# A two-layer decoder trunk on one core: eight small products of the gates and of the compressed keys, each set in one run on TensorE

## The chip, the core and the metric

The kernel runs on one core of a Trainium2 chip. Its engines work side by side, each through its own list of instructions in order: TensorE (PE in the profile; its loads of weights stand apart as PEld), VectorE (DVE), ScalarE (ACT), GpSimd (POOL), and SyncE (SP), which here only issues loads and stores. The metric is the device time of one execution in microseconds (us); less is better. The profile comes from one further execution, recorded instruction by instruction.

## What is computed

The input is x with 512 positions of 1024 numbers, all in float32. Layer 0 normalises x, projects it once, and feeds the columns to two groups of heads: a chunked mLSTM with 4 heads, and a sparse attention with 8 query heads in two groups. Layer 1 is a gated linear recurrence. Two small parts of layer 0 matter here. The first is the gates of the mLSTM, which per chunk of 128 positions need a running maximum of the input gate over the decayed forget gate:

```
bcum = jnp.cumsum(fj, axis=-1)
D = jnp.where(causal, bcum[..., :, None] - bcum[..., None, :] + ij[..., None, :], -jnp.inf)
inter = bcum + m[..., None]
m_row = jnp.maximum(jnp.max(D, axis=-1), inter)
...
m_new = jnp.maximum(bL + m, jnp.max(dl, axis=-1))
```

The second is the compressed keys and values of the attention, two small matrices behind each other with a GELU between them:

```
def compress(blocks, w1, w2):
    flat = blocks.reshape(*blocks.shape[:3], CMP_LEN * NSA_HEAD_DIM)
    return jax.nn.gelu(flat @ w1) @ w2
...
k_cmp = compress(heads(kc, G)[:, :, cmp_idx] + ck_pos, ck_w1, ck_w2)
k_cmp = partial_rope(rms_norm(k_cmp, k_norm[0]), cmp_end)
v_cmp = compress(heads(vc, G)[:, :, cmp_idx] + cv_pos, cv_w1, cv_w2)
```

## The kernel before

The large projections take most of PE's time. Each float32 operand is split into a high and a low part (`whi`, `wlo` for weights, `h0h`, `h0l` for activations), and a product is three PE products of 128 x 128 weights with 512 columns: high by high, high by low, low by high. They add up in PSUM tiles named `mm` (three of them). Weights come from memory in 512 KB pieces (`raw`), ACT rounds a piece to `whi`, DVE subtracts to get `wlo`; there are four buffers of each, so a new piece is converted when PE has left an old one.

The work around the projections hangs in generators, one for each small task. `cg_evac` takes the first group of columns (compressed keys and gates) out of PSUM and starts `kc_t`, `compress` and `gates`. `nq_evac` and `nkv_evac` take out queries and keys and start `prep_q(i)` and `prep_k(i)` for each block i of 128 positions: squares on ACT (`sqj`), a root on POOL (`qrs`, `krs`), a scaling and a rotation on DVE (`x`), four transposes on PE, and the split into high and low parts (`q`, `kd`). `cmp_sm(i)` multiplies the queries of block i with the compressed keys (`kcd`) and makes a softmax of the scores (`sc`, `ce`).

The two tasks that the change touches are these. In `gates()` (line 1117) the scans over `ar` leave running maxima in `rows` (the half `cmx`), and `mrow` holds the carried maximum of the four chunks. `Mr`, the other half of `rows`, is the larger of the two, in lines 1157 to 1159 with one step on DVE for each chunk. Then lines 1169 to 1172 put five products into the PSUM tile `gp`: `on4` by `bd` (32 columns), and four that turn `Mr` into columns (4 rows deep, 128 weight columns, 4 moving columns). In `compress()` (line 1052) `hk` and `h4`, both in the buffer `gb`, are the outputs of the GELU, and lines 1078 to 1081 multiply them with `w2`: one product of 64 weight columns for the keys, two of 128 for the values of two groups. A float32 product that isn't split takes two passes on PE. Both tasks, the transposes of `prep_q` and `prep_k` and others share the two PSUM buffers `tp`. Behind the products come `Mc` (out of `gp`), and `kr`, `vbk`, `kn`, `kh` and `kcd` (the keys on their way to the scores).

No engine runs the program in the order in which it is written. `Plan` records every operation with a price, and `Plan.schedule` sorts each stage six times by these prices, by what an operation waits for, and by how urgent it is; the best order is then issued from line 408. So all instructions carry line 408 in the profile, and they are told apart by the names of their tiles. Products may be tied: lines 249 to 257 set `a.next = b` for two PE products written one behind the other if they fill the array from different columns on with the same load, and the scheduler then issues `b` right behind `a`. The first of a chain takes over what the others wait for. The eight products above were not tied.

Of the kernel before, what the change touches and what calls it, by code (L numbers as in the profile page):

```python
# [158 lines left out]

class Op:  # L160
    __slots__ = ("eng", "fn", "a", "k", "cost", "acc", "pred", "succ", "left", "ready", "start", "end", "done", "late", "after",
                 "load", "cols", "idx", "first", "tiles", "tab", "next")


class Plan:
# [37 lines left out]
    def add(self, eng, fn, a, k, cost):  # L203
        o = Op()
        o.eng, o.fn, o.a, o.k, o.cost, o.idx = eng, fn, a, k, cost, len(self.ops)
        o.pred, o.succ, o.acc, o.tiles, o.first = {}, {}, [], [], []
        o.tab = self.TAB.get(a[2]) if eng == "A" and len(a) > 2 else None
        o.load, o.cols = k.pop("_pe", (0.0, ()))
        o.after = k.pop("_after", None)
        o.next = None  # L210
        aps = [(x, j == 0) for j, x in enumerate(a) if isinstance(x, bass.AP)]
        aps += [(x, n == "accum_out") for n, x in k.items() if isinstance(x, bass.AP)]
        for x, w in aps:
            n = x.tensor.name
            if n in self.tag:
                o.acc.append((n, *((1, 0, 1) if n[:3] in PSUMS else self.region(x)), w))
        self.ops.append(o)


    def edges(self):  # L220
        for o in self.ops:
            for n, m, p0, p1, w in o.acc:
                h = self.hist.get(n)
                if h is None:
                    h = self.hist[n] = []
                if n not in self.tag:
                    pass
                elif n not in self.born:
                    o.first.append(n)
                    self.order.setdefault(self.tag[n], []).append(n)  # L230
                    self.born[n] = o
                elif self.born[n] is not o:
                    o.pred.setdefault(self.born[n], -self.born[n].cost)
                for q, qm, q0, q1, qw in h:
                    if q is not o and (w or qw) and q0 < p1 and p0 < q1 and qm & m:
                        raw = qw and not w
                        lat = self.LAT[q.eng] if raw or q.eng != o.eng else 0.0
                        if q.eng == "T" == o.eng:
                            lat = -q.cost
                        o.pred[q] = max(o.pred.get(q, lat), lat)  # L240
            for n, m, p0, p1, w in o.acc:
                h = self.hist[n]
                if w:
                    h[:] = [x for x in h if x[1] & ~m or x[2] < p0 or x[3] > p1]
                h.append((o, m, p0, p1, w))
            o.tiles = list({x[0] for x in o.acc if x[0] in self.tag})
            if o.after is not None:
                o.pred.setdefault(o.after, -o.after.k.get("_ns", 0.0))
        for a, b in zip(self.ops, self.ops[1:]):
            if a.eng == "T" == b.eng and len(a.cols) < 4 and a.load == b.load and a.cols[0] < b.cols[0]:  # L250
                a.next = b
        for b, a in list(zip(self.ops, self.ops[1:]))[::-1]:
            if b.next:
                for q, lat in a.pred.items():
                    if q is not b:
                        b.pred[q] = max(b.pred.get(q, lat), lat)
                a.pred = {b: -b.cost}
        for o in self.ops:
            for q, lat in o.pred.items():
                q.succ[o] = lat  # L260
# [168 lines left out]
class Mark:  # L429
    t = None  # L430
# [186 lines left out]
def build(tc, I, out):  # L617
# [6 lines left out]
    with ExitStack() as ctx:  # L624
# [42 lines left out]
        def cut(t, shape, p=slice(0, 128)):  # L667
            n = 1
            for d in shape:
                n *= d  # L670
            v = t[p, :n]
            if len(shape) == 1:
                return v
            ls = "abcdef"[:len(shape)]
            return v.rearrange("p (" + " ".join(ls) + ") -> p " + " ".join(ls), **dict(zip(ls, shape)))
# [284 lines left out]
        with ExitStack() as c0:  # L960
# [91 lines left out]
            def compress():  # L1052
# [25 lines left out]
                T.matmul(p[:64, :64], hk, w2[:, 0, :], start=True, stop=True, skip_group_check=True)  # L1078
                for g in range(2):
                    T.matmul(p[:, 64 + 64 * g:128 + 64 * g], flat(h4[:, g]), w2[:, 1, :], start=True, stop=True,  # L1080
                             skip_group_check=True)
                b_end()
                kr = s_t("kr", [64, 64], 1)
                V.tensor_copy(kr, p[:64, :64])
# [32 lines left out]
            def gates():  # L1117
# [36 lines left out]
                V.tensor_copy(aL, cust(cmx, [[128, 4]], 127))  # L1154
                V.tensor_tensor_scan(mrow[:, 1:5], aL, bL, 0.0, op0=OP.max, op1=OP.add)
                Mr = rows[:, 1, :]
                for t in range(4):
                    V.tensor_scalar(Mr[:, 128 * t:128 * (t + 1)], cmx[:, 128 * t:128 * (t + 1)], mrow[:, t:t + 1], None,
                                    op0=OP.max)
                ML = s_t("ML", [4, 2, 4], 1)  # L1160
                V.tensor_tensor(ML[:, 0, :], aL, mrow[:, :4], op=OP.max)
                V.tensor_copy(ML[:, 1, :], mrow[:, :4])
# [6 lines left out]
                T.matmul(gp[:, 16:48], on4, flat(bd), start=True, stop=True, skip_group_check=True)  # L1169
                for t in range(4):  # L1170
                    T.matmul(gp[:, 4 * t:4 * t + 4], Mr[:, 128 * t:128 * (t + 1)], shc("id", 4, 4),
                             start=True, stop=True, skip_group_check=True)
                Mc = s_t("Mc", [128, 48], 1)
                V.tensor_copy(Mc, gp[:, :48])
                V.scalar_tensor_tensor(ex[:, :16], aa, LNS, Mc[:, 16:32], op0=OP.add, op1=OP.subtract)
# [960 lines left out]
```

## Time and profile before

| what | us |
|---|---|
| timed runs, median of 3 | 616.07 (616.03 to 616.64) |
| the profiled execution | 618.45 |
| its span, first to last instruction | 616.7 |
| PE busy in the span | 608.3 (99%) |
| DVE busy | 456.9 (74%) |
| ACT busy | 332.4 (54%) |
| POOL busy | 106.2 (17%) |

The profiled execution takes somewhat longer than the timed ones. Its span leaves out what lies before the first and behind the last instruction. A product counts as busy until its last column has left the array, while the next has long begun; how fast PE works is read from the distance between starts.

### The profile page before, as it was taken

To read this page: it belongs to the slowest core of one execution; us is meant where nothing else is said; L and a number is where in the kernel's file an instruction comes from. 1 tells how busy PE (TensorE), PEld (TensorE's weight loads), DVE (VectorE), ACT (ScalarE), POOL (GpSimd) and SP (SyncE) were. 2 spreads that over 40 slices of the span, in tenths; PEclk is the share of its full clock that TensorE was granted. 3 is DMA by queue.
4 is the path that set the end of the run, shared out by engine and by line. 5 is a ranking of instruction groups with operands and counts; after the bars stand their busy time and mean duration, and the time that the engine had idled before them with its cause. 6 is when DMAs were issued, how large, how long until landed. Compare 5 with 4: busy or idle time off the path is not lost.

```text
span 616.7 us, 11759 instructions
## 1 busy us (share of the span) xinstructions
PE 608.3 (99%) x4482; PEld 490.4 (80%) x4482; DVE 456.9 (74%) x980; ACT 332.4 (54%) x870; POOL 106.2 (17%) x143
## 2 busy tenths in 40 slices
PE   8999999999999999999999999999999999999997
PEld 8877787877778777888888887788877877788886
DVE  5876998698899766566745679997588798996441
ACT  7564465667777664373534756446527365565300
POOL 1441532102002002063012111023000100122100
PEclk9997999999999999999999999999999999999999
DMA  8723133809409407925343524473222215473111
GB/s 321 262 107 103 51 98 127 338 4 222 189 18 299 95 2 179 238 72 213 96 160 120 170 72 135 132 231 118 69 71 70 70 39 168 142 281 126 35 73 64
DMA packets 23528, 82.91 MB, mean 134 GB/s; under 512 B 3376, under 2 KB 4272, under 8 KB 20656
## 3 DMA queue, kind: packets, MB, share of 16 engines
q1 hardware_dynamic: 20880, 65.09, 32.1%
q0 software_dynamic: 2304, 16.78, 10.4%
q8 instruction: 35, 0.57, 0.4%
q10 hardware_dynamic: 288, 0.30, 0.2%
q14 instruction: 21, 0.17, 0.1%
HBM read 77.96 MB, written 20.97 MB: 160 GB/s over the span
## 4 chain that ended last, share of the span: by engine, by line
PE 89%; DVE 5%; issue 2%; DMA 1%; POOL 1%; ACT 1%; DVEq 0%; ACTq 0%; POOLq 0%
PE mm L408 32%; PE mx L408 18%; PE my L408 15%; PE sc L408 7%; PE ac L408 5%; PE tp L408 5%; PE tq L408 5%; PE sd L408 2%; DMA raw<-in_wall_dram 1%; DVE wlo L408 1%; DVE x L408 1%; POOL qk L408 1%; DVE ce L408 0%; POOL krs L408 0%; DVE q L408 0%
## 5 line engine op out<-in xcount | busy, mean ns | idle before, releaser
L408 ACT ACTIVATE whi<-raw 128x512 fp32r<-128x512 f32 (+1 forms) x184 | 104.9, 615 | 83.2 <-PE my L408 30.1
L408 DVE TENSOR_TENSOR wlo<-raw,whi 128x1024 fp32r<-128x1024 f32 (+1 forms) x96 | 114.3, 1197 | 33.0 <-ACT whi L408 32.7
L408 PE MATMUL mm<-whi,h0l 128*128 128x512 f32 (+1 forms) x168 | 68.3, 407 | 0.0
L408 PE MATMUL mm<-whi,h0h 128*128 128x512 f32 (+1 forms) x168 | 68.2, 409 | 0.0
L408 PE MATMUL mm<-wlo,h0h 128*128 128x512 f32 (+1 forms) x168 | 68.0, 409 | 0.0
L408 ACT ACTIVATE PP<-sc,nm 128x256 f32<-128x256 f32 (+3 forms) x56 | 30.7, 549 | 20.7 <-DVE nm L408 18.8
L408 DVE CUSTOM_DVE_ANT_0 sc<-sc,cz 128x384 f32<-128x384 f32 (+3 forms) x64 | 31.1, 504 | 13.4 <-PE sc L408 10.6
L408 PE MATMUL mm<-h0h,whi 128*128 128x512 f32 x96 | 38.9, 407 | 0.0
L408 PE MATMUL mm<-h0h,wlo 128*128 128x512 f32 x96 | 38.5, 401 | 0.0
L408 PE MATMUL mm<-h0l,whi 128*128 128x512 f32 x96 | 38.4, 400 | 0.0
L408 PEld LDWEIGHTS mm<-whi,h0l 128*128 128x128 f32 x168 | 32.3, 193 | 6.4 <-issue 0.2
L408 PEld LDWEIGHTS mm<-wlo,h0h 128*128 128x128 f32 x168 | 32.3, 193 | 5.9 <-issue 0.2
L408 PEld LDWEIGHTS mm<-whi,h0h 128*128 128x128 f32 x168 | 32.4, 193 | 5.4
L408 DVE TENSOR_TENSOR HB<-HB,tt 128x512 f32<-128x512 f32 x48 | 31.8, 686 | 3.8 <-PE sd L408 2.5
L408 POOL TENSOR_TENSOR ivgg<-ivgg,zz 128x256 f32<-128x256 f32 x16 | 16.5, 1032 | 67.7 <-ACT zz L408 67.7
L408 ACT ACTIVATE PT<-tp 128x384 f32<-128x384 f32 (+1 forms) x48 | 23.4, 525 | 8.0 <-PE tp L408 7.8
L408 PE MATMUL sc<-kd,q 128*128 128x256 f32 (+2 forms) x112 | 27.4, 339 | 0.0
L408 POOL TENSOR_SCALAR held<-wlo 128x1 f32<-128x1 f32 x16 | 4.5, 282 | 127.8 <-DVE wlo L408 122.6
L408 PE MATMUL my<-h1l,whi 128*128 128x512 f32 x64 | 25.9, 404 | 0.0
L408 PE MATMUL my<-h1h,whi 128*128 128x512 f32 x64 | 25.8, 404 | 0.0
L408 PE MATMUL mx<-h1h,whi 128*128 128x512 f32 x64 | 25.7, 402 | 0.0
L408 PE MATMUL my<-h1h,wlo 128*128 128x512 f32 x64 | 25.7, 401 | 0.0
(379 smaller groups left out, 1566.7 us busy)
## 6 DMA issues: line engine op xcount, KB each, us to landing
raw<-in_wall_dram SPq DMA_DIRECT2D x76, 512.0 KB, 3.8
wt<-in_wall_dram POOLq DMA_DIRECT2D x12, 1024.0 KB, 9.9
raw<-wt SPq DMA_DIRECT2D x16, 512.0 KB, 3.8
wt<-wt POOLq DMA_DIRECT2D x4, 1024.0 KB, 15.8
bias<-in_brow_dram SPq DMA_DIRECT2D x9, 256.0 KB, 4.7
xt<-in_xt_dram SPq DMA_DIRECT2D x8, 256.0 KB, 5.4
w<-in_cw_dram SPq DMA_DIRECT2D x2, 1024.0 KB, 9.3
x<-in_xt_dram SPq DMA_DIRECT2D x2, 1024.0 KB, 6.8
```

The lines of the kernel that those rows point to most:

```text
L408: o.fn(*o.a, **k)
```

## The change

Three edits in the kernel and one in the planner. An operation may carry `_join`; two neighbours on PE are then tied whatever columns they fill. The two `h4` products carry it, and so do the four products of `Mr`: `hk` and the two `h4` products become one chain, `bd` and the four of `Mr` another. `Mr` itself is made in one DVE step, the larger of two tensors, with `mrow` read 128 times for each chunk.

```diff
+        o.join = k.pop("_join", False)
...
-            if a.eng == "T" == b.eng and len(a.cols) < 4 and a.load == b.load and a.cols[0] < b.cols[0]:
+            if a.eng == "T" == b.eng and (b.join or len(a.cols) < 4 and a.load == b.load and a.cols[0] < b.cols[0]):
                 a.next = b
...
                 T.matmul(p[:64, :64], hk, w2[:, 0, :], start=True, stop=True, skip_group_check=True)
                 for g in range(2):
                     T.matmul(p[:, 64 + 64 * g:128 + 64 * g], flat(h4[:, g]), w2[:, 1, :], start=True, stop=True,
-                             skip_group_check=True)
+                             skip_group_check=True, _join=True)
...
                 Mr = rows[:, 1, :]
-                for t in range(4):
-                    V.tensor_scalar(Mr[:, 128 * t:128 * (t + 1)], cmx[:, 128 * t:128 * (t + 1)], mrow[:, t:t + 1], None,
-                                    op0=OP.max)
+                V.tensor_tensor(cut(Mr, (4, 128), slice(0, 4)), cut(cmx, (4, 128), slice(0, 4)),
+                                cust(mrow, [[1, 4], [0, 128]]), op=OP.max)
...
                 T.matmul(gp[:, 16:48], on4, flat(bd), start=True, stop=True, skip_group_check=True)
                 for t in range(4):
                     T.matmul(gp[:, 4 * t:4 * t + 4], Mr[:, 128 * t:128 * (t + 1)], shc("id", 4, 4),
-                             start=True, stop=True, skip_group_check=True)
+                             start=True, stop=True, skip_group_check=True, _join=True)
```

The planner makes a new order of the whole first layer from this. The numbers of instructions stay the same on PE, ACT, POOL and SP; DVE has three fewer. PE's order differs at some 40 places within its first third, most of them between the products themselves and the first attention scores.

On PE, the place of the products in the order before, from the second product with `gb` on (`tp` is the shared PSUM buffer, `w` holds `w2`, `on4` the ones):

```order
L408 MATMUL tp_189<-w2_96,gb_162 128x64
L408 MATMUL mm_198<-wlo_138,h0h_85 128x512
L408 MATMUL tp_196<-bd_169,on4_170 128x32
L408 MATMUL mm_198<-whi_137,h0h_85 128x512
L408 MATMUL tp_196<-cs_68,rows_165 128x4
L408 MATMUL mm_198<-whi_137,h0l_86 128x512
L408 MATMUL tp_196<-cs_68,rows_165 128x4
L408 MATMUL mm_198<-wlo_138,h0h_85 128x512
L408 MATMUL tp_196<-cs_68,rows_165 128x4
```

and in the new order, from the last of six 512-column products that stand behind the transpose of `gb`:

```order
L409 MATMUL mm_198<-wlo_138,h0h_85 128x512
L409 MATMUL tp_189<-bd_169,on4_170 128x32
L409 MATMUL tp_189<-cs_68,rows_165 128x4 x4
L409 MATMUL tp_191<-w2_96,gb_162 64x64
L409 MATMUL tp_191<-w2_96,gb_162 128x64 x2
L409 MATMUL mm_198<-whi_137,h0h_85 128x512
```

Two chains stand in one piece, the gates' ahead of the keys', with no projection between them.

On DVE, what makes the operands, before (`aL` and `mrow` are the carried maxima, `ML` and `bd` their diagonal form):

```order
L408 COPY aL_167<-rows_165 4x4
L408 SCALAR_TENSOR_TENSOR mrow_166<-aL_167,bL_160 4x4
L408 TENSOR_TENSOR ML_168<-aL_167,mrow_166 4x4
L408 COPY ML_168<-mrow_166 4x4
L408 SCALAR_TENSOR_TENSOR gb_162<-gb_162 128x128
L408 TENSOR_TENSOR bd_169<-ML_168,cs_68 4x32
L408 TENSOR_SCALAR rows_165<-rows_165,mrow_166 4x128 x2
L408 TENSOR_SCALAR gb_162<-tp_174 128x256
L408 TENSOR_SCALAR rows_165<-rows_165,mrow_166 4x128 x2
```

and now:

```order
L409 COPY aL_167<-rows_165 4x4
L409 SCALAR_TENSOR_TENSOR gb_162<-gb_162 128x128
L409 SCALAR_TENSOR_TENSOR mrow_166<-aL_167,bL_160 4x4
L409 TENSOR_TENSOR rows_165<-rows_165,mrow_166 4x512
L409 TENSOR_TENSOR ML_168<-aL_167,mrow_166 4x4
L409 COPY ML_168<-mrow_166 4x4
L409 TENSOR_TENSOR bd_169<-ML_168,cs_68 4x32
L409 TENSOR_SCALAR gb_162<-tp_174 128x256
```

The third step on `gb` moves ahead of `mrow`, and the step that fills `rows` ahead of `bd`.

On PE, where the compressed keys are turned and first used, before (`kh` is the key chain's last tile on DVE):

```order
L408 MATMUL tp_223<-cs_68,kh_195 128x64
L408 MATMUL mm_222<-wlo_200,h0h_85 128x512
L408 MATMUL mm_220<-whi_213,h0h_87 128x512
L408 MATMUL mm_220<-whi_213,h0l_88 128x512
L408 MATMUL mm_222<-whi_201,h0h_87 128x512
L408 MATMUL mm_222<-whi_201,h0l_88 128x512
L408 MATMUL sc_227<-kcd_94,q2_203 128x64 x4
L408 MATMUL sc_227<-kcd_94,q2_204 128x64 x3
L408 MATMUL tp_238<-cs_68,x2_210 128x128
L408 MATMUL sc_227<-kcd_94,q2_204 128x64
```

and now:

```order
L409 MATMUL tp_222<-cs_68,kh_197 128x64
L409 MATMUL mm_223<-whi_199,h0h_85 128x512
L409 MATMUL mm_223<-whi_199,h0l_86 128x512
L409 MATMUL mm_223<-wlo_200,h0h_85 128x512
L409 MATMUL mm_223<-whi_201,h0h_87 128x512
L409 MATMUL mm_223<-whi_201,h0l_88 128x512
L409 MATMUL mm_220<-wlo_202,h0h_87 128x512
L409 MATMUL sc_224<-kcd_94,q2_203 128x64 x4
L409 MATMUL sc_224<-kcd_94,q2_204 128x64 x4
L409 LDWEIGHTS idb_126
```

The scores of block 0 stand in one piece, five 512-column products earlier than before, and the transposes of `x` for block 2 (`x2_210`) have left it: they stand behind fourteen more, nine later than their first one did.

## Rows read from the trace of the kernel before

**Rows 1.** The page: granted clock of PE by slice, and the chain's shares.

```profile
PEclk9997999999999999999999999999999999999999
PE 89%; DVE 5%; issue 2%; DMA 1%; POOL 1%; ACT 1%; DVEq 0%; ACTq 0%; POOLq 0%
```

**Rows 2.** Timeline of PE, undisturbed: start us, length us, operation, operands, shapes.

```profile
57.54 0.39 PE L408 MATMUL mm<-whi,h0l 128*128 128x512 f32 x1
57.77 0.39 PE L408 MATMUL mm<-wlo,h0h 128*128 128x512 f32 x1
```

**Rows 3.** Timeline of PE at the place of the change, 43 to 48 us.

```profile
43.45 0.40 PE L408 MATMUL mm<-wlo,h0h 128*128 128x512 f32 x1
43.98 0.30 PE L408 MATMUL tp<-cs,gb 128*128 128x128 f32 x1
44.04 0.48 PE L408 MATMUL mm<-whi,h0h 128*128 128x512 f32 x1
44.36 0.39 PE L408 MATMUL mm<-whi,h0l 128*128 128x512 f32 x1
...
46.10 0.47 PE L408 MATMUL mm<-wlo,h0h 128*128 128x512 f32 x1
46.50 0.40 PE L408 MATMUL tp<-bd,on 4*128 4x32 f32 x2
46.84 0.50 PE L408 MATMUL mm<-whi,h0h 128*128 128x512 f32 x1
...
47.58 0.49 PE L408 MATMUL mm<-whi,h0l 128*128 128x512 f32 x1
```

**Rows 4.** Timeline of PE, where the slow stretch begins and ends.

```profile
49.05 0.71 PE L408 MATMUL mm<-whi,h0h 128*128 128x512 f32 x1
...
56.19 0.39 PE L408 MATMUL mm<-whi,h0h 128*128 128x512 f32 x1
```

**Rows 5.** Busy time by stretch: length, PE, PEld, DVE, ACT, POOL, clock, DMA share, GB/s.

```profile
30.00:44.00 14.00, 13.82 (x124) 11.23 (x122) 10.15 (x34) 9.53 (x42) 5.41 (x6) 1.00 0.36 140
44.00:49.00 5.00, 5.00 (x24) 3.41 (x24) 4.72 (x13) 2.27 (x5) 0.77 (x1) 1.00 0.00 0
...
51.00:55.90 4.90, 4.90 (x12) 3.76 (x12) 0.64 (x4) 1.03 (x2) 0.19 (x1) 0.50 0.39 115
```

**Rows 6.** Loads of weights of the four-row products: least, median, most ns; timeline.

```profile
L408 PEld LDWEIGHTS tp<-cs,rows x8: 181/184/332, 47.3 to 49.9; 4*128 4x128 f32 x8
...
47.27 0.29 PEld L408 LDWEIGHTS tp<-cs,rows 4*128 4x128 f32 x2 [0.25 <-issue]
```

**Rows 7.** Timeline of PE, small products in one piece (x counts passes).

```profile
36.07 0.34 PE L408 MATMUL tp<-cs,lf 128*4 128x1 f32 x8
36.34 3.71 PE L408 MATMUL sc<-w,cT 128*64 128x128 f32 x64
```

**Rows 8.** Timeline of DVE: the operands, a step of two tensors, the keys.

```profile
43.23 0.15 DVE L408 TENSOR_TENSOR_SCAN mrow<-aL,bL 4x4 f32<-4x4 f32 x1
...
43.87 0.47 DVE L408 TENSOR_SCALAR rows<-rows,mrow 4x128 f32<-4x128 f32 x2
...
45.31 1.27 DVE L408 TENSOR_TENSOR x<-qk,qrs 128x512 f32<-128x512 f32 x2
...
60.51 0.22 DVE L408 COPY kh<-kn 64x128 f32<-64x128 f32 x1
```

**Rows 9.** Timeline of PE, its two waits between 40 and 130 us, in brackets.

```profile
67.84 0.33 PE L408 MATMUL tp<-cs,x 128*128 128x128 f32 x1 [0.97 <-DVE x L408]
...
101.19 0.66 PE L408 MATMUL tp<-cs,x 128*128 128x128 f32 x4 [0.60 <-ACT vp L408]
```

**Rows 10.** Busy time by stretch, columns as in rows 5.

```profile
51.70:56.05 4.35, 4.35 (x12) 3.38 (x11) 0.00 (x1) 1.15 (x2) 0.00 (x0) 0.51 0.35 113
56.05:85.00 28.95, 27.98 (x149) 23.11 (x148) 26.43 (x62) 17.66 (x78) 12.17 (x12) 1.00 0.21 64
85.00:103.00 18.00, 17.40 (x92) 14.20 (x91) 16.80 (x47) 8.21 (x33) 5.79 (x8) 1.00 0.50 161
```

More of the change, by code (lines that the diff above doesn't have):

```diff
@@ L161 @@
     __slots__ = ("eng", "fn", "a", "k", "cost", "acc", "pred", "succ", "left", "ready", "start", "end", "done", "late", "after",
-                 "load", "cols", "idx", "first", "tiles", "tab", "next")
+                 "load", "cols", "idx", "first", "tiles", "tab", "next", "join")
 class Plan:
```

## The prediction

> **What bounds the kernel now.** Start with the page [rows 1]: TensorE (PE) carries 89% of the chain that ended last, so a change pays only where it shortens what PE does or waits for. The line of the granted clock has one dip, in the fourth slice. So the next view is PE's timeline there, and the first thing to fix is a yardstick: where nothing disturbs it, one 512-column product follows another after 0.23 us [rows 2]. "Big" means such a product below.
>
> Then PE's timeline at the place of the change [rows 3]. It waits 0.30 us ahead of the transpose of `gb` (43.45 + 0.23 = 43.68, to 43.98). Behind that, the eight small products of `compress()` and `gates()` each stand alone between two bigs. With a four-row product the pair takes 0.74 us (46.84 to 47.58) against 0.23 for the big alone: 0.51 extra, though the product has four columns. PE never shows as idle there, so no list of waits has this loss; only the distance of the starts shows it.
>
> Third, the clock [rows 4, 5]. From 44 to 49 us PE is busy all of 5.00 us at clock 1.00 (2.4 GHz) in just this alternation; right behind it the clock falls to 0.50 (1.2 GHz), stays there while PE runs dense bigs again, and is back by 56 us. From 49.05 to 56.19 lie 15 bigs and one small product; at full clock they take 15 x 0.23 + 0.51 = 3.96 us and took 7.14. The fall costs 3.18 us, more than the alternation.
>
> **The change part by part.** Sums are made on the profiled execution (618.45 us, span 616.7) and carried to the median of the timed runs, 616.07. That those have the same fall of the clock is an assumption; they agree within 0.1%.
>
> *The run on PE.* In the new order six bigs follow the transpose of `gb`, then `bd`, the four `rows` products and the three of `gb` in one piece, and bigs again. What does a small product cost inside a run? No row shows a four-row product behind another, so I put it together. Its two passes load 128 columns each; one load takes 181 ns and two together 0.29 us, so the second starts 0.11 behind the first [rows 6]. Five gate products of two loads: 5 x 0.215 = 1.08. The two wide ones of `gb` load as much, 0.43; for the 64-wide one I put 0.15, a little over half of 0.215 for half the columns. Into the run: 46.10 to 46.50 is 0.40, a big and 0.17 more. Out of it: `bd` starts 0.34 ahead of its big (46.50 to 46.84), 0.12 more than its loads, and that big's own load lies open, 0.09 (44.04 is followed at 0.32 in place of 0.23). Sum over the bigs: 0.17 + 1.08 + 0.43 + 0.15 + 0.12 + 0.09 = 2.04 us.
>
> From 43.45 to 56.19 before are 12.74 us and 25 bigs. After: 25 x 0.23 = 5.75, the transpose 0.15 (its 0.06 to the next big and that big's open load), the run 2.04: 7.94. The difference, 4.80, is 0.30 (the wait), 1.32 (the run) and 3.18 (the clock, if it stays up). Bounds for the run: at 0.51 each it gains nothing; at the pitch of the cheapest row, eight passes of one column in 0.34 us [rows 7], sixteen passes are 0.7 and the gain is 2.7. I take 1.32, since loads of this very shape are the nearest row.
>
> *Are the operands there?* A run starts when all of its operands should be there, so its first product could hold PE, and every product queued on PE behind it. By the starts PE reaches it at 43.68 + 0.06 + 0.32 + 5 x 0.23 = 45.21. On VectorE (DVE) the third step on `gb` moves ahead of `mrow`, to 43.23 at the earliest [rows 8], which is what takes the 0.30 wait away. Then come `mrow`, the new single step for `Mr`, two `ML`, `bd`. The new step joins two tensors over 512 columns: the `x` step of that form takes 0.64 (two in 1.27), against 0.47 for each pair of the four old ones. `bd` is then ready near 44.7, half a us ahead of PE; the operand of the `gb` products near 45.25, a us ahead of their turn. The run waits for nothing. DVE saves 0.3, on no path here and counted at nothing; if the half us of cover were gone, each tenth of delay would count in full.
>
> *Does the clock stay up?* Shown are two lulls without a fall: 72 passes of small products in one piece from 36.07 to 40.05 us, in a stretch at clock 1.00 [rows 5, 7], and 0.97 of idle time for `x` in a stretch at 1.00 [rows 9, 10]. The run with its 2.04 us is more like these than like six us of alternation. I take the clock as kept, 3.18; the other end is zero.
>
> *What the new order does later.* The key chain behind the run (`kr`, `kn`, `kh`, `kcd`) and the transposes of `x` move against the bigs, and the score products of one block hardly alternate with the transposes any more. PE waits twice there before: 0.97 for `x`, 0.60 for `vp` [rows 9]. `x` for query block 2 now stands 9 bigs (2.1 us) later on PE, so this wait may go even with PE 4.8 us early; the second may stay, or a new one come, since DVE has less room. Between no gain, with new waits of like size, and all 1.57, I take 0.5. DVE is the limit of all this: its idle time is 4.35 us while PE is slow, 28.95 - 26.43 = 2.52 up to 85 and 18.00 - 16.80 = 1.20 up to 103 [rows 10], 8.07 us in all. PE can be early by no more than that, and the forecast asks for 5.3 of it.
>
> PE's last two thirds and all of layer 1 on every engine stand in the order of before, and the chain runs over PE there, so the lead should last. On SP and POOL two neighbours swap places here and there: nothing. Sum: 616.07 - 4.80 - 0.5 = 610.77, say **610.8 us**.
>
> **The rivals.**
>
> *The clock falls all the same* (0.14). Then the alternation isn't what brings it down, the 3.18 stays, and 616.07 - 0.30 - 1.32 = 614.4 results. For it: one fall in one trace is thin evidence of a cause, and the run is still 2 us of light work. Against it: the two lulls named above. The same time results if the timed runs have no fall to lose. The Trainium skill, page "TensorE: Matmul & The Clock Gate", section "Why this matters for your kernels", warns of idle gaps between bursts of matmuls as what drops the clock; by that rule a PE without idle time wouldn't lose it, and the change wouldn't win it back. The trace disagrees: busy 5.00 of 5.00 us right ahead of the fall.
>
> *DVE takes it back* (0.10). If DVE can't use the 4.35 us, because its work then waits on weights whose buffers PE frees, only the 3.72 behind 56 us are left, and new waits on `x` or `kcd` of about a us: a gain near 2.6, 613.5. Against it: that idle time is there because PE freed buffers slowly, and PE frees them faster now.
>
> *Nothing* (0.07). Each product of the run costs its 0.51, and the clock falls: 616.07 - 0.30, near 615.8.
>
> *Slower* (0.04). The place is the transpose of `kh`, which PE now reaches 44 bigs and two runs of transposes behind the run, near 45.21 + 2.04 + 44 x 0.23 + 0.7 = 58.1. DVE ended `kh` at 60.73 before, 4.35 idle us among it [rows 8, 10]; without them 56.4, a cover of 1.7 us. If `kh` comes late by the cover and 1.6 us more, PE's idle time brings the clock down there (3.18) and the 4.80 is gone; from there on the kernel is slower. With 3 us of wait and one more of 0.97 at the next block: 616.07 - 4.80 + 3.18 + 3 + 0.97 = 618.4.
>
> **How the numbers follow.** Forecast 0.65, and the rivals as given. The forecast's own range: with all later waits gone and a run at two thirds of its estimate 616.07 - 4.80 - 1.57 - 0.7 = 609.0; with a new wait of one us 612. The range goes on to the clock's rival, 614.4, and leaves out some 0.15. A measurement of this kernel can tell about 0.2%, 1.2 us. Faster by more than that: the forecast, DVE's rival and most of the clock's, 0.87; within it 0.08; slower 0.05.
>
> **What would show it.** Right: the eight products in one piece on PE's timeline, some 2 us long, beginning near 45.2 without a wait; the 25th big from 43.45 over near 51.4; no stretch at 0.50 between 40 and 70 us; DVE without its idle 4.35. Wrong: a wait ahead of `bd`; clock 0.50 after 47 us; a wait above 1 us on `kcd`, `kh` or `x` between 58 and 95 us; or a lead at 56 us that is gone by 260.

## The result and the profile after

The changed kernel takes 611.88 us (median of 6 runs, 611.45 to 613.49) where the kernel before takes 616.05 (6 runs, 614.98 to 617.24): a ratio of 0.9934, with a 95% interval from 0.9918 to 0.995. That is 4.2 us less, inside the range of the prediction and 1.1 us above its value. The profiled execution took 611.6 us with a span of 609.8, against 618.45 and 616.7 before. So the profiles differ by 6.9 us and the timed medians by 4.2, and this difference needs explaining as much as the gain does. Three single executions far above all others (663.91 us in e1, 843.22 in e3, 1193.92 of before) stand in the medians given below, but in no ratio and in no count of falls.

The page of after, granted clock by slice and shares of the chain, to be held against [rows 1]:

```profile
PEclk9999999999999999999999999999999999999999
...
PE 92%; DVE 5%; DMA 1%; issue 1%; ACT 0%; DVEq 0%; ACTq 0%
```

The dip of the fourth slice is gone. PE's timeline at the place of the change (start us, length us, operation, operands), to be held against [rows 3]:

```profile
43.45 0.40 PE L409 MATMUL mm<-wlo,h0h 128*128 128x512 f32 x1
43.68 0.27 PE L409 MATMUL tp<-cs,gb 128*128 128x128 f32 x1
...
44.96 0.40 PE L409 MATMUL mm<-wlo,h0h 128*128 128x512 f32 x1
45.29 0.40 PE L409 MATMUL tp<-bd,on 4*128 4x32 f32 x2
45.53 1.03 PE L409 MATMUL tp<-cs,rows 4*128 4x4 f32 x8
46.49 0.92 PE L409 MATMUL tp<-w,gb 128*64 128x64 f32 x6
47.22 0.48 PE L409 MATMUL mm<-whi,h0h 128*128 128x512 f32 x1
47.53 0.40 PE L409 MATMUL mm<-whi,h0l 128*128 128x512 f32 x1
...
51.48 0.40 PE L409 MATMUL mm<-whi,h0h 128*128 128x512 f32 x1
51.71 0.49 PE L409 MATMUL tp<-cs,x 128*128 128x128 f32 x3
```

There is no wait ahead of the transpose of `gb`. The run begins at 45.29 without a wait, and the next big starts at 47.22. Inside it a four-row product takes 0.24 us (0.96 for four, 45.53 to 46.49), against 0.51 beyond its big when it stood alone. The big that started at 56.19 before [rows 4], the 26th from the one at 43.45 on, starts at 51.48: 4.71 us of lead.

Busy time by stretch (length, PE, PEld, DVE, ACT, POOL, clock, DMA share, GB/s). The first fence is after, the second, for the same two stretches, before:

```profile
43.00:56.00 13.00, 13.00 (x69) 10.63 (x68) 11.86 (x33) 7.54 (x30) 2.96 (x5) 1.00 0.31 90
56.00:104.00 48.00, 47.69 (x245) 39.47 (x244) 43.47 (x109) 26.03 (x100) 17.85 (x21) 1.00 0.35 112
```

```profile
43.00:56.00 13.00, 12.86 (x45) 9.08 (x44) 8.20 (x26) 4.01 (x9) 3.17 (x4) 0.74 0.28 82
56.00:104.00 48.00, 46.42 (x244) 38.14 (x242) 44.23 (x113) 26.89 (x113) 17.96 (x20) 1.00 0.32 99
```

In the first 13 us the clock is 1.00 where it was 0.74, and DVE works 11.86 us of 13 where it worked 8.20: the idle 4.35 us of [rows 10] have been used. In the second stretch PE stands idle for 0.31 us where it stood idle for 1.58 (48 less 46.42).

That 0.31 is one wait, on a stretch shown further below (e8). The waits of 0.97 us for `x` and 0.60 for `vp` [rows 9] are gone. So the profiles' 6.9 us are 4.71 up to the first transposes of `x`, 1.26 in the waits behind (0.97 + 0.60 - 0.31), and some 0.9 later, of which 0.4 is one wait for `Sx` (0.7 before, 0.3 after) and the rest isn't placed.

### The profile page after: what moved, and what is told of

The parts are those of the page before. It is cut to its first block, busy times and chain, and to the rows that moved or that the text cites. A ratio compares the mean times of both kernels' runs of the same rounds, so it can differ in the third digit from the quotient of the medians.

```text
span 609.8 us, 11750 instructions
## 1 busy us (share of the span) xinstructions
PE 603.1 (99%) x4482; PEld 488.3 (80%) x4482; DVE 456.7 (75%) x977; ACT 331.2 (54%) x870; POOL 105.6 (17%) x143
## 4 chain that ended last, share of the span: by engine, by line
PE 92%; DVE 5%; DMA 1%; issue 1%; ACT 0%; DVEq 0%; ACTq 0%
PE mm L409 34%; PE mx L409 18%; PE my L409 15%; PE sc L409 8%; PE tp L409 5%; PE ac L409 5%; PE tq L409 5%; PE sd L409 2%; DMA raw<-in_wall_dram 1%; DVE x L409 1%; DVE wlo L409 1%; DVE q L409 1%; DVE HB L409 0%; DVE AL L409 0%; ACT whi L409 0%
## 5 line engine op out<-in xcount | busy, mean ns | idle before, releaser
L409 PE MATMUL mm<-whi,h0l 128*128 128x512 f32 (+1 forms) x168 | 66.8, 397 | 0.0
L409 PE MATMUL mm<-wlo,h0h 128*128 128x512 f32 (+1 forms) x168 | 66.4, 400 | 0.0
L409 ACT ACTIVATE PP<-sc,nm 128x256 f32<-128x256 f32 (+3 forms) x56 | 30.7, 549 | 22.5 <-DVE nm L409 20.7
```

The costliest lines, as they stand in the source:

```text
L409: o.fn(*o.a, **k)
```

## The experiments

One number serves for all kernels below, the **extra time**. Take PE's timeline from the start of the last big ahead of the transpose of `gb` to the start of the first transpose of `x`, and subtract 0.232 us for each big in between. Before: 43.45 to 56.65 are 13.20 us, with 27 bigs (6.26), so 6.95 extra. After: 43.45 to 51.71 are 8.26, with 26 bigs (6.02), so 2.24. Where the clock is at 0.50 (1.2 GHz), a big takes 0.427 in place of 0.232, so a stretch at that level costs 0.457 of its length. The last column leaves this out. The 0.232 is 3.95 us for 17 bigs in after (47.53 to 51.48); the 0.427 is 4.27 us for ten in before, between these two:

```profile
51.22 0.63 PE L408 MATMUL mm<-whi,h0h 128*128 128x512 f32 x1
...
55.49 0.63 PE L408 MATMUL mm<-whi,h0l 128*128 128x512 f32 x1
```

| Kernel | What differs | Extra, us | At 0.50 for, us | Extra less that |
|---|---|---|---|---|
| before | | 6.95 | 6.8 | 3.8 |
| e1 | before again | 5.45 | 3.4 | 3.9 |
| e3 | before, two runs | 2.74 | none | 2.7 |
| e4 | before, one step for the rows | 4.93 | 3.4 | 3.4 |
| after | | 2.24 | none | 2.2 |
| e5 | after again | 2.21 | none | 2.2 |
| e2 | after, all eight apart | 6.62 | 6.8 | 3.5 |
| e9 | after, gates' five apart | 6.62 | 6.8 | 3.5 |
| e6 | after, two keys apart | 2.22 | none | 2.2 |
| e7 | after, wait of 1.48 us | 5.35 | 3.4 | 3.8 |
| e10 | after, wait of 0.75 us | 4.60 | 3.4 | 3.0 |
| e11 | after, four steps for the rows | 2.77 | none | 2.8 |
| e8, e12 | after, other places in runs | 2.23, 2.25 | none | 2.2 |

The experiments ran in three groups, each on one chip beside its own runs of before: e1 to e4 (before 616.82, median of 34 runs), e5 to e8 (616.36, 18 runs), e9 to e12 (615.73, 29 runs).

A profile shows one execution, but every execution of these kernels comes with its mean granted clock. In the profiles a mean of 0.994 goes with a fall of 6.8 us, 0.996 with one of 3.4, and 0.999 or 1.000 with none. No profile has 0.997 or 0.998; by their times the first is counted with the falls here, the second with the others.

| Kernels | Executions | With a fall |
|---|---|---|
| before (three groups and e1) | 91 | 57, six of them at 0.993 or 0.994 |
| e2, e9, e4 (alternation) | 12, 12, 12 | 8, 8, 9 |
| e7, e10 (wait ahead of the run) | 12, 12 | 8, 7 |
| after (first comparison and e5) | 6, 7 | 1, 0 |
| e3, e6, e8, e11, e12 | 10, 6, 6, 12, 6 | none |

Of before's executions, those without a fall have a median of 615.2 us, those at 0.996 or 0.997 one of 617.0, the six at 0.993 or 0.994 one of 618.5. So alternation or a wait makes a fall frequent but not certain, and what decides it in one execution stays open.

### e1: the kernel before, again

No edit.

> The kernel before, unchanged, to see the time and the mean granted clock of each of its executions side by side. The profiled execution of before took 618.45 us at a mean clock of 0.994, 2.4 us over the median of the timed runs (616.05), and that of after 611.6 us at 1.000. Theory A (the fall of the clock at the alternating products differs from execution to execution, and the profiled one was long): the median is 615.5 to 616.7 us, most executions show a mean clock of 0.996 to 0.999, and the time follows the clock, with the ones at 0.994 near 618 us; the fall then costs some 1 us in a typical execution, not the 3.2 us of the profile. Theory B (the profiled execution was longer for other reasons): the clock is 0.994 in all of them while their times spread from 615 to 617 us. Rival C (the clock does not fall in typical executions at all): a mean clock of 1.000 at 616 us, so that the gain of the change came without the clock.

Measured: a median of 616.79 us (12 runs); its profiled execution took 616.59 us, at a mean clock of 0.996. A stretch of PE's timeline in it:

```profile
49.12 0.38 PE L408 MATMUL tp<-cs,rows 4*128 4x4 f32 x2
...
50.00 0.58 PE L408 MATMUL mm<-whi,h0h 128*128 128x512 f32 x1
50.38 0.63 PE L408 MATMUL mm<-whi,h0l 128*128 128x512 f32 x1
```

And its busy time from there on (columns as above):

```profile
50.10:53.40 3.30, 3.30 (x10) 2.53 (x9) 1.14 (x6) 0.00 (x0) 0.64 (x2) 0.50 0.73 231
```

The fall is there, from 50.0 us on, behind the last small product (in the profile before it began at 49.2, ahead of the last one at 49.69), but it lasts half as long: 3.4 us in place of 6.8. The stretch costs 1.6 us here and 3.1 in the profile that the prediction was made on. That is theory A, with the median 0.1 us above its range, and in part rival C: by the second table over a third of before's executions have no fall, two of the eleven of e1 among them (615.09 and 615.36 us). The timed runs of before go from 614.34 to 619.68 us over the three groups.

### e2: the changed kernel with the eight apart

The order in which the planner's result is issued is changed for PE alone (`small` are the eight products, `pe` is PE's list, `new` what is issued in its place):

```diff
+        i, new = pe.index(small[0]), list(pe)
...
+        big = pe[i + 8:i + 15]
+        new[i:i + 15] = [x for p in zip(small, big) for x in p] + small[7:]
...
-        for o in sorted(self.ops, key=lambda o: (o.start, o.idx)):
+        for o in self.place(sorted(self.ops, key=lambda o: (o.start, o.idx))):
```

> The changed kernel with one thing undone: TensorE's order at the small products. Each of the eight (`bd`, four `rows`, three keys) has one big of those that follow the run behind it, as before; every other instruction, on every engine, stands as in the changed kernel, the one VectorE step included. Theory A (the alternation itself costs about 1.3 us, and it brings the clock down): 611.9 + 1.3 + 1 to 3.2 for the fall, 614.2 to 616.4 us, with a mean clock of 0.994 to 0.998 and its low stretch beginning at about 48 to 50 us. Rival B (the alternation costs its 1.3 us, but the clock fell for another reason, such as the wait ahead of the keys' transpose): 613.0 to 613.5 us at 1.000. Rival C (the gain comes from the planner's order behind the run and from the VectorE step): 611.5 to 612.3 us at 1.000.

Measured: 615.27 us (12 runs, 613.46 to 617.49), a ratio to before of 0.9978 (0.9959 to 0.9997); profiled 616.45 us at a clock of 0.994. PE's timeline:

```profile
46.93 0.50 PE L446 MATMUL mm<-wlo,h0h 128*128 128x512 f32 x1
47.36 0.38 PE L446 MATMUL tp<-cs,rows 4*128 4x4 f32 x2
47.67 0.49 PE L446 MATMUL mm<-whi,h0h 128*128 128x512 f32 x1
48.10 0.38 PE L446 MATMUL tp<-cs,rows 4*128 4x4 f32 x2
48.41 0.60 PE L446 MATMUL mm<-whi,h0l 128*128 128x512 f32 x1
48.94 0.48 PE L446 MATMUL tp<-w,gb 128*64 128x64 f32 x2
```

The pairs take 0.74 us again, and the clock falls to 0.50 for 6.8 us:

```profile
48.70:55.40 6.70, 6.70 (x19) 5.28 (x19) 4.40 (x14) 1.31 (x4) 0.88 (x2) 0.50 0.50 152
```

Theory A: the order on PE alone, with all other engines as in after, brings back both losses, the fall in 8 of 12 executions. By the first table the alternation costs 1.3 us (3.5 less 2.2) and the fall 3.1 in this execution. The waits for `x` and `vp` haven't come back, so they aren't due to the alternation.

### e3: the kernel before with two runs

On PE alone, mark 1 being the keys' products, 2 `bd` and 3 the `rows`:

```diff
+        for m in ((1,), (2, 3)):
+            run = [o for o in small if o.mark in m]
...
+            i = new.index(run[-1])
...
+            new = [o for o in new[:i] if o not in run] + run + new[i + 1:]
```

> The kernel before with one thing done: on TensorE the three keys' products stand in one run, and the gates' five in another, each at about the place where the last of them stood, and the bigs between them are moved ahead. Nothing else differs from the kernel before: the four VectorE steps for the rows, the order of the other engines and all that follows. Theory A: the alternation's cost goes but for one more way into a run and out of it (about 0.3 us), so 1.0 us, and the clock stays at 1.000, 1 to 3.2 us more; the waits of 0.30, 0.97 and 0.60 us that before has at the keys' transpose and behind stay. 611.9 to 614.0 us, at 1.000. Rival B (the clock fell for another reason): 614.7 to 615.2 us at 0.994 to 0.998. Rival C (the order and the VectorE step make the gain): 615.7 to 616.3 us.

Measured: 614.18 us (11 runs, ten of them from 613.44 to 616.31), a ratio of 0.9961 (0.9942 to 0.9981); profiled 613.49 us at a clock of 1.000. PE's waits (us in total, times, longest):

```profile
PE tp L448 <- DVE x L448: 1.0, 1, 1.0
...
PE tp L448 <- ACT vp L448: 0.6, 1, 0.6
```

Theory A on the clock: nothing but PE's order at eight products differs from before, and the fall is gone, here and in all ten executions, with 2.7 us extra in place of 3.8 and more. The median is 0.2 us above theory A's range. The waits behind are all there. They and the 0.5 us more at the place (2.74 less 2.24) make up 1.8 of the 1.9 us by which this profile's span (611.7) is longer than after's.

### e4: the one VectorE step alone

```diff
-                for t in range(4):
-                    V.tensor_scalar(Mr[:, 128 * t:128 * (t + 1)], cmx[:, 128 * t:128 * (t + 1)], mrow[:, t:t + 1], None,
-                                    op0=OP.max)
+                V.tensor_tensor(cut(Mr, (4, 128), slice(0, 4)), cut(cmx, (4, 128), slice(0, 4)),
+                                cust(mrow, [[1, 4], [0, 128]]), op=OP.max)
```

> The kernel before with the rows' operand made in one VectorE step (0.68 us in the changed kernel, for four of about 0.23 us) and neither run: the planner lays the order out anew and still puts bigs between most of the small products (`bd` and the first key stand together, so seven single places instead of eight). Theory A: the wait of 0.30 us at the keys' transpose goes, one place of alternation goes (about 0.15 us), the clock falls as before: 615.0 to 616.0 us at 0.994 to 0.998. Rival B (VectorE's length sets the time here): 612.0 to 613.5 us, with the clock at 1.000. Rival C (a new order makes new waits): 616.3 us or more.

Measured: 614.71 us (12 runs, 611.75 to 616.14), a ratio of 0.9956 (0.9936 to 0.9975); profiled 614.73 us at 0.996, with a fall of 3.4 us. Faster than I expected of theory A, and not for rival B's reason, since the clock fell, in 9 of 12 executions. The list of PE's waits in this kernel:

```profile
PE ac L408 <- POOL hm L408: 1.0, 1, 1.0
PE sc L408 <- ACT h0h L408: 0.8, 1, 0.8
PE tq L408 <- DVE Sx L408: 0.7, 1, 0.7
PE sc L408 <- DVE h0l L408: 0.4, 1, 0.4
PE tq L408 <- DVE HB L408: 0.2, 1, 0.2
```

The wait at the transpose of `gb` and those for `x` and `vp` are gone, 1.87 us in all (0.30 + 0.97 + 0.60). So the step, with the order that the planner makes of it, carries this part, and the joins carry the rest (whether by its time or by that order, see the later waits below). With 2.1 us under its group's before, it is worth about as much as the two runs of e3 (2.6).

### e5: the changed kernel, again

No edit.

> The changed kernel, unchanged, beside the kernel before on one chip, with more executions of each. So far before shows 616.6 us at a mean clock of 0.996 and 618.45 at 0.994 in two profiles, and timed runs from 614.5 to 619.7; after 611.6 at 1.000. Theory A (the clock's fall in before is of two lengths at least, and after has none): after has a median of 611.4 to 613 us, a clock of 1.000 in the profile, and a gain over before of 4.0 to 5.5 us. Rival B (after falls as often as before, the first profile was a lucky one): a profile at 0.994 to 0.997, and a gain of 2 to 3 us.

Measured: 613.11 us (7 runs, 611.69 to 613.90), 3.25 us under before in its group, a ratio of 0.9943 (0.9923 to 0.9962). Theory A expected 4.0 to 5.5, so it missed, though the clock doesn't fall at the run (2.21 extra, none at 0.50 there). Its profiled execution was one of the longer ones, 613.9 us with a span of 612.1, and the trace shows why. PE's timeline near the start, here e5, then after:

```profile
9.39 0.44 PE L409 MATMUL sc<-whi,h0l 128*128 128x288 f32 x1
9.63 0.44 PE L409 MATMUL sc<-wlo,h0h 128*128 128x288 f32 x1
...
10.04 0.30 PE L409 MATMUL sc<-wlo,h0h 128*128 128x288 f32 x1
```

```profile
8.67 0.30 PE L409 MATMUL sc<-whi,h0l 128*128 128x288 f32 x1
8.81 0.29 PE L409 MATMUL sc<-wlo,h0h 128*128 128x288 f32 x1
```

Up to 9.87 us e5's products of 288 columns stand 0.24 us apart, where after's stand 0.13 apart from 6.2 us on, but for a wait. That is about the ratio that a big has between the two levels (0.427 to 0.232), but the profile's row of the clock shows 1.00 in this stretch, so a lower clock as the reason isn't shown. The last big ahead of the transpose of `gb` starts at 44.66 in place of 43.45, 1.2 us late. The other 1.1 us of this execution lie behind, 0.8 of them in two waits (`kT` 0.4, and `Sx` 0.7 in place of 0.3). The start varies in both kernels, then (before and e1 are 0.36 us apart at this big, 43.45 and 43.09), and spreads the times of each.

### e6: two keys apart

```diff
-                             skip_group_check=True, _join=True)
+                             skip_group_check=True)
                 b_end()
```

> The changed kernel with the joining of the keys' products alone undone, the planner laying the order out anew: `bd`, the four `rows` and the first key stand in one run, and the second and third key each have a big ahead. A smaller dose of alternation, two single places within 1 us. Theory A (what it costs is a sum over places, and so short an alternation leaves the clock alone): 0.1 to 0.2 us for each place (in before the keys' three places stand 0.37 us apart beyond their bigs, where the run has 0.24), so 0.2 to 0.4 us over after, 611.8 to 612.6, at 1.000. Rival B (any single small product brings the clock down): 2 to 4 us over after, 613.5 to 616, at 0.994 to 0.997.

Measured: 612.90 us (6 runs, 611.78 to 613.81) beside 613.11 for after; no fall. Of the rivals A is right on the clock, but its 0.1 to 0.2 us a place is wrong: the extra time is 2.22, as in after. PE's timeline shows it:

```profile
46.18 0.33 PE L409 MATMUL tp<-w,gb 128*64 128x64 f32 x2
46.44 0.51 PE L409 MATMUL mm<-whi,h0h 128*128 128x512 f32 x1
46.78 0.33 PE L409 MATMUL tp<-w,gb 128*128 128x64 f32 x2
46.92 0.48 PE L409 MATMUL mm<-whi,h0l 128*128 128x512 f32 x1
47.24 0.33 PE L409 MATMUL tp<-w,gb 128*128 128x64 f32 x2
```

From 46.78 to 47.24, a key and a big, are 0.46 us, so the key costs 0.23 beyond its big. In after's run the three cost 0.73, 0.24 each. A key's product with its 128 rows loses nothing by standing alone. (The expectation's 0.37 us in before is the first key alone, 44.91 to 45.51; the second took 0.22, 45.51 to 45.96.)

### e7 and e10: a wait ahead of the run

The memset of `on4`, which `bd` reads, is issued again ahead of `bd`, eight times in e7 and five times in e10 (`fill`), while GpSimd has nothing else to do; `small[0]` is `bd`.

```diff
+        fill = next(o for o in seq if o.mark == 9)
+        i = seq.index(small[0])
+        return seq[:i] + [fill] * 8 + seq[i:]
```

> The changed kernel with a wait put ahead of the run: on GpSimd, which is free there, the memset of `on4`, the operand of `bd`, is issued eight more times (0.19 us each in the profile, from about 44.9 us on), so that TensorE stands idle for some 1.0 to 1.4 us before `bd`. All else is the same. Theory A (lost time on TensorE counts in full, and one wait of this length leaves the clock alone; it is the many small products with their weight loads that bring it down): 1.0 to 1.4 us over after, 612.6 to 613.5 us at 1.000. Rival B (it is idle time that brings the clock down, of which the alternation is only one form): 1.0 to 1.4 us and the fall, 1.5 to 3.5 us: 614.2 to 616.8 us at 0.994 to 0.997. Rival C (the wait is taken back by the later waits, which VectorE and ScalarE then have time to finish ahead of): 611.8 to 612.3 us.

> The changed kernel with a shorter wait ahead of the run: the memset of `on4` issued five more times instead of eight (0.245 us each in e7), which should leave TensorE idle for 0.6 to 0.8 us instead of 1.48. Theory A (the clock falls only when the lost time in the stretch is large enough; a small loss costs itself and no more): 0.6 to 0.8 us over after, 612.5 to 613.9, at 0.999 or 1.000. Rival B (the run of eight small products together with any visible wait brings it down): the fall as in e7, 614.2 to 616 us at 0.996 or 0.997.

Measured: e7 615.18 us (12 runs, 612.88 to 616.36) beside 613.11 for after, profiled at 0.996; e10 613.91 us (12 runs, 611.65 to 614.77), profiled at 0.996. In e10 on PE's timeline:

```profile
44.66 0.40 PE L418 MATMUL mm<-wlo,h0h 128*128 128x512 f32 x1
45.81 0.40 PE L418 MATMUL tp<-bd,on 4*128 4x32 f32 x2 [0.75 <-POOL on L418]
46.05 1.03 PE L418 MATMUL tp<-cs,rows 4*128 4x4 f32 x8
47.01 1.16 PE L418 MATMUL tp<-w,gb 128*64 128x64 f32 x6
47.93 0.77 PE L418 MATMUL mm<-whi,h0h 128*128 128x512 f32 x1
48.50 0.63 PE L418 MATMUL mm<-whi,h0l 128*128 128x512 f32 x1
```

And its busy time behind the run (columns as above):

```profile
47.60:50.90 3.30, 3.30 (x10) 2.72 (x10) 0.93 (x4) 1.15 (x2) 0.00 (x0) 0.50 0.55 159
```

My theory A fell in both. The waits count in full (1.48 us in e7, where the extra less the fall rises by 1.55; 0.75 in e10, where it rises by 0.8), and in each profile the clock goes to 0.50 behind the run, for 3.4 us. Rival B is right on the clock: idle time ahead of the run does what the alternation did. It doesn't do it every time: 4 executions of e7 and 5 of e10 have a mean clock of 0.999 or 1.000 (e10's lowest, 611.65, at 1.000), and so e10's median lies 0.3 us under rival B's range.

### e8 and e12: the same idea at other places

e8: PE's four single transposes of `x` near 75 us go behind the products of `kcd` and `q`. e12: the same, and the four products of `acc` near 22.5 us stand together. (`one` are the four transposes, `end` the big behind the mask's product.)

```diff
+        new = [o for o in pe if o not in one]
+        i = new.index(end)
+        new[i:i] = one
```

> The changed kernel with the same idea at another place: at 75.2 us of its profile four transposes of `x` stand one by one between the products of `kcd` and `q`, with a wait of 0.31 us ahead of the first. Here the eight `kcd` products and the mask's product stand together, and the four transposes in one run behind them. Theory A (the place costs its wait and some 0.1 us for each of four single transposes, and nothing is late behind): 0.5 to 0.8 us under after, 611.0 to 611.5. Rival B (the transposes' readers are late by as much and TensorE waits for them a little later): the same time as after, with a new wait of about 0.5 us between 76 and 100 us.

> The kernel of e8 with one more place done in the same way: at 22.5 us of the profile of after four products of one column (`acc`) stand one by one between bigs, 0.45 us from one big to the next where 0.23 is usual; here the four stand together, and nothing else differs from e8. Theory A: 0.3 to 0.6 us under e8 (four times 0.22, less the run itself), and so 0.7 to 1.0 us under after; e8 had 611.7 beside 613.1 for after on one chip, so 611.2 to 612.3 by the chip. Rival B (the stretch behind waits for VectorE's or ScalarE's results, which come no sooner): the same as e8, with a new wait behind 24 us.

Measured: e8 611.70 us (6 runs, 610.88 to 612.25), a ratio of 0.9925 (0.9906 to 0.9945); e12 611.73 (6 runs, 611.01 to 612.97), 0.9925 (0.9903 to 0.9947) in its own group. PE's timeline of after, then of e8, at the place:

```profile
74.60 0.39 PE L409 MATMUL mm<-whi,h0l 128*128 128x512 f32 x1
...
75.77 0.30 PE L409 MATMUL tp<-cs,x 128*128 128x128 f32 x1 [0.31 <-DVE q L409]
...
76.91 0.48 PE L409 MATMUL mm<-wlo,h0h 128*128 128x512 f32 x1
```

```profile
74.59 0.39 PE L458 MATMUL mm<-whi,h0l 128*128 128x512 f32 x1
...
76.54 0.48 PE L458 MATMUL mm<-wlo,h0h 128*128 128x512 f32 x1
```

The place is 0.36 us shorter (2.31 to 1.95), most of it the wait of 0.31, and no wait has come behind it up to 104 us. Less than theory A asked for: these are 128-row products again, and lose little by standing apart. The median is 1.4 us under after's in the group, but e8's and e5's intervals overlap and after's start differs from execution to execution, so only the 0.36 is shown. e12 adds nothing: from the big ahead of the four `acc` products to the fifth big behind are 2.06 us in it and 2.05 in after. Together these products of one column and 128 rows cost 0.2 us each, as they did apart.

### e9 and e11: the gates' join, and the joins without the step

```diff
-                             start=True, stop=True, skip_group_check=True, _join=True)
+                             start=True, stop=True, skip_group_check=True)
```

> The changed kernel with the joining of the gates' products alone undone, the planner laying the order out anew: the three keys stand in one run, and `bd` and the four `rows` have a big between each two. Five single places, between the two of e6 (no fall of the clock) and the eight of e2 (a fall). By the kernel before, the gates' places stand 0.74 us apart, so each costs 0.51 where the run has 0.24: 5 times 0.27 is 1.3 us, less about 0.2 for the run's own way in and out. Theory A (it is the time that TensorE loses in this stretch that brings the clock down, whether by a wait, as the 1.48 us of e7 did, or by places of alternation): 1.1 us and the fall, of 1.7 or 3.4 us: 614.5 to 616.5 us, at 0.994 to 0.997. Rival B (it takes the whole alternation of 4 us, as in before): 1.0 to 1.3 us over after and no fall, 612.9 to 614.0, at 0.999 or 1.000.

> The changed kernel with the rows' operand made in four VectorE steps again, as before; both joins stand, and the planner lays the order out anew (it puts one big between the keys' run and the gates' run). Theory A (the one step on VectorE is what takes away the waits at the keys' transpose and, behind, of 0.97 us for `x` and 0.60 us for `vp`, which e4, with that step alone, had lost and e3, with the two runs alone, still had): those waits are back, 1.2 to 1.9 us over after, 613.5 to 615.0, with the clock at 0.999 or 1.000. Rival B (the joins' order takes them away as well): 611.7 to 613.1 us and no wait over 0.4 us between 56 and 104 us.

e11 takes back the single VectorE step for `Mr` (e4's diff the other way round).

Measured: e9 614.38 us (12 runs, 611.79 to 615.96), 0.9959 (0.9938 to 0.9979), profiled at 0.994 with 6.8 us at 0.50: theory A (the median 0.1 us under its range). The last column is that of e2, 3.5, though the keys stand in one run here, so the gates' five four-row products carry the whole cost of the alternation (3.5 less 2.2, 1.3 us, 0.26 each). e11: 614.98 us (12 runs, 614.16 to 617.57), 0.9984 (0.9969 to 1.0), profiled at 0.999. Two of PE's waits in e11:

```profile
PE tp L409 <- DVE x L409: 1.0, 1, 1.0
...
PE tp L409 <- DVE kd L409: 0.8, 1, 0.8
```

Theory A: the wait for `x` is back, with another for `kd` in place of `vp`, and 0.15 us at the transpose of `gb`. The clock doesn't fall in any of its 12 executions. Without the one VectorE step the joins are worth 0.75 us here, under what a measurement of this kernel can tell.

## Why the prediction was right, and where it wasn't

**The run.** Predicted 2.04 us over the bigs; from 45.19 (the last big's end by the yardstick) to 47.22 and 0.08 for the open load, 2.11. It started without a wait, 0.08 later than reckoned. With the 0.30 us of wait the prediction asked for 1.62 here; 3.8 less 2.2 is 1.6. The terms were right and the reason half right: the sum gave the three keys a part of the saving, and e6 (for two of them) and e9 beside e2 (for all three) show that they have none. What loses by standing alone is the four-row product, 0.51 against 0.24; for a 128-row product it is 0.23 against 0.24.

**The clock.** Predicted kept, and it is, in 12 of 13 executions of after; one timed run of 613.49 us has a mean clock of 0.997, and no profile shows where it fell. That the alternation was the cause is shown by e2 and e3 from both sides, and by the counts: a fall in 40 of 60 executions of the kernels with alternation or a wait, in 1 of 53 of those with the small products in runs and no wait ahead. Two things said beside it were wrong. First, the step that carried the 3.18 us to the timed runs on an assumption failed: the fall lasts 6.8 us in the profile that I read, as in 6 of 91 executions of before, 3.4 in e1, and 34 of the 91 have none. The 2.4 us by which that profile's execution was longer than the timed median were the sign. Of the timed 4.2 us some 2.9 are, by the profiles, the wait, the run and the later waits (1.62 + 1.26), which leaves 1.3 for the clock and all else. The mean clocks agree with it in size: the median of before less that of its executions without a fall is 1.6, 1.3 and 0.4 us in the three groups. The lowest runs agree too: 614.34 before and 611.45 after, in different groups, are 2.9 apart. Second, I took two lulls without a fall as a sign that idle time and a run are harmless. Each alone is: the waits of 0.97 us in before and e3 stayed at 1.00, and so did after's run. The two together aren't (e7, e10). In the first table every profile with a fall has a larger last column than every profile without one; that is an order among these profiles, and no more is read from it.

The Trainium skill, page "TensorE: Matmul & The Clock Gate", section "Why this matters for your kernels", names idle gaps between bursts of matmuls as what drops the clock, and the prediction said that the trace disagrees. e7 and e10 agree with its direction, though their waits, 1.48 and 0.75 us with a run of small products behind, are shorter than the gaps that the section warns of; before and e2 show that it isn't the whole of it, since there the clock falls with PE shown as busy throughout.

**The later waits.** Predicted 0.5, between 0 and 1.57; measured 1.26. The term was mis-sized: the prediction saw that the transposes of `x` for block 2 stand nine bigs later on PE, and gave this and all else behind the run 0.5. e4 and e11 show that the single step, with the order the planner lays out for it, takes away the wait at `gb` and the ones for `x` and `vp`, 1.9 us. The traces speak for the order and not for the 0.3 us of VectorE time that the prediction counted at nothing: where the four steps stand (before, e1, e3, e11) the transposes of `x` that waited come 61 or 62 bigs behind the transpose of `gb` and wait about 1 us, where the one step stands (after, e2, e4, e6, e9) they come 70 bigs behind and don't wait. VectorE's order differs there as well, and no run has the one step in the old order, so which part of the new order does it stays open. The cover at `kh` held: DVE ends it at 56.35, PE reaches it at 58.50, 2.1 us of cover where 1.7 were reckoned.

**The rivals.** DVE didn't take the lead back: it used the idle 4.35 us, and PE waits 0.31 us in all from 56 to 104. The clock's rival and the one on `kh` didn't come about, but e7 and e10 show that the clock's was nearer than its chance says: a wait of 0.75 us ahead of the run does it in 7 of 12 executions.

**The sum.** 1.9 too much for the clock (3.18 for 1.3) and 0.8 too little for the later waits (0.5 for 1.26) make the 1.1 us by which 610.8 was too low. Two misses of opposite sign partly cancel, so the nearness of the value is in part luck; the 1.3 is what the other terms leave over, and wasn't measured by itself.

## What to carry to other kernels

Before a loss in one profile is carried to a median, take a second profile and read the mean clock of every timed execution: the fall of the clock here was twice as dear in the profile that I read as in the next, and over a third of the executions had none. Where small products have few rows, put them in one run and keep what they read ready ahead of it, since even a wait of 0.75 us in front of the run brought the fall of the clock back in 7 of 12 executions; products with all 128 rows may stand where the schedule wants them. And ask of every instruction saved on a second engine which order the planner will make of it: the step whose time was counted at nothing was worth nearly half of the gain, by the order that came with it.

## What was not expected of the hardware

- A product of four rows costs 0.51 us between 512-column products and 0.24 among its like; products of 128 rows with 64 columns (0.23 and 0.24) or with one column (0.22 and 0.20) cost the same in both places.
- The granted clock fell to 0.50 behind a run of 2.1 us with 0.75 us of idle time ahead of it (e10's profile; by the mean clock in 7 of 12 executions), and did not behind the run alone (after's and e5's profiles) nor behind an idle 0.97 us alone (before, e3).
- One kernel's executions differ: of 91 of before, 34 show no fall in their mean clock, 51 one like e1's of 3.4 us, six one like the first profile's of 6.8.
- At the start the lower pace (0.24 us for a 288-column product, against 0.13) was over by 6.2 us in one execution of the same kernel and lasted to 9.9 in another, 1.2 us of difference by 43 us. The profile's clock shows 1.00 there in both.
